# Sparse attention's first query units in float32, its modulation row formed in the feed-forward stages, the residual update in the head loop, and new planner costs

## The chip, the cores and the metric

The kernel runs on one core of one Trainium2 chip, as one launch. The metric is the device time of that launch in microseconds (us), lower is better. One core has a matrix engine (PE; its weight loads are listed as PEld), a vector engine (DVE), a scalar engine (ACT), a general engine (POOL), and a sync engine (SP) whose queue starts the transfers (DMA) from main memory (HBM). PE reads its operands from the on-chip buffer SBUF and adds into the accumulator PSUM.

## The reference, cut to what matters

Two networks in a row on 256 tokens of width 1024. The first has two layers with modulation and post-norm; the second has four layers with pre-norm (two of them forgetting attention, "fox", one gated linear attention, "gla", one gated delta net, "gdn").

```python
def first_block(x, c, ada_w, ada_b, ...):
    cond = silu(c)
    for i in range(2):
        mod = cond @ ada_w[i] + ada_b[i]                 # 6 rows of 1024
        sh1, sc1, gt1, sh2, sc2, gt2 = split(mod, 6)
        hin = x * (1 + sc1) + sh1
        y = rwkv7_time_mix(hin, ...) if i == 0 else dsa_attention(hin, ...)
        x = layernorm(ALPHA * x + (1 + gt1) * y, ln_g[i, 0], ln_b[i, 0])
        hin = x * (1 + sc2) + sh2
        x = layernorm(ALPHA * x + (1 + gt2) * swiglu(hin, ...), ln_g[i, 1], ln_b[i, 1])

def dsa_attention(h, ...):                               # sparse attention
    q, ckv, q_idx, k_idx, w_idx = split(h @ w_in)
    score = einsum(w_idx, relu(q_idx . k_idx)), causal
    idx = top_k(score, 64)                               # of 256 keys
    p = softmax((q w_uk) . ckv[idx] / 8 + rel_bias)      # 16 heads
    return ((p ckv[idx]) w_uv) @ w_out

def gdn_mixer(x, ...):                                   # 4 query/key, 8 value heads, chunks of 64
    q, k, v, z, b, a = split(x @ w_in)                   # q, k, v through a causal convolution and silu
    # decayed delta rule by chunks: the inverse of a triangular matrix of k k^T, then q k^T with the state
    return (rms_norm(o) * silu(z)) @ w_out
```

## The kernel before

**A planner inside the program.** The functions below don't issue instructions: each adds an operation to `Prog` (L346), with its possible engines and a cost in ns for each (L538 for ACT, L565 for two-input operations, L671 for copies). `schedule()` then plays all engines forward by these costs, gives every operation an engine and a buffer, and the instructions are emitted on each engine in the planned order. What order and engine an operation gets is thus decided by costs, priorities (`prog.pri`: a higher number goes later) and free buffers. Most large tiles, among them the raw weights `raw`, the split weights `whl`, the float32 inputs `xraw` and the rows `lrgb`, share one pool of 18 slots of 8 KB per partition.

**Weight units.** The token side is held transposed (features on partitions, 256 tokens in the free dimension). `ws` (L730s) makes 256 output features from a unit of 1 MB of weights: one DMA `raw`, two casts to the fp32r type (`whl<-raw`, L667 on ACT or L671 on POOL), two subtractions on DVE that give the low parts (`whl<-raw,whl`, L677), then 48 matmuls of 128x256 in three passes (high x high, high x low, low x high). `ws_full` does the same unit in plain float32: 16 matmuls straight from `raw` and the float32 input `xraw`, with no cast and no subtraction (the trace lists each float32 matmul as two). `as_proj` is the other form (512 output columns at a time) used for the projections at the end of a stage; with `turn` the two halves of the columns are computed one after the other.

**Stages**, in program order, with their place in the trace: rwkv to 262 us; its projection and layernorm to 284; feed-forward 0 to 476 (`ffi0` to 368, `ffo0` behind it); sparse attention (`dsa`) 476 to 600; layernorm 600 to 634; feed-forward 1 634 to 800; fox 835 to 931; gla 954 to 1049; gdn 1049 to 1207; fox 1226 to 1321; the last projection to 1366.

**Modulation.** `ada(l, g)` (L878) forms two rows of 1024 of `mod`, half by half: per half 8 DMAs of 512 KB (`adaraw`) and 8 DVE operations of 128x1024 (`adaacc`), then a sum over partitions on PE (`adaps`) and one small DVE operation (`adab`). `ada(1, 2)` gives `sc2` and `gt2` of layer 1, with priority 500, and is called just ahead of `dsa`.

**Sparse attention.** A projection gives scores' inputs; eight pairs of small matmuls `ix`, ACT's relu `rl` and DVE's weighted sum `dw` give the score; eight rounds of MAX8 and MATCH_REPLACE8 on DVE, for two blocks of tokens, rank it and leave the mask `selm`. Beside this, PE makes the first two query units (`d_q`), the values `vev` and the keys `kal`. The head loop (k = 0 to 7, two heads each) then adds the mask to the logits (`lgt<-selm,identb`), forms softmax on DVE, ACT and POOL (`hw`), transposes (`pT`) and multiplies (`op`); at k = 4 the query units 2 and 3 are put in, and PE goes on to the projection `do` where the heads leave room. `flush` (before the first `d_q` unit) runs the residual update of the layernorm before: four DVE operations of 128x1024 (`xr<-...,lrgb`).

**gdn.** `n_q` has eight units (0, 1 queries; 2, 3 keys; 4 to 7 values); each goes through a convolution on DVE and ACT (`cu`, `nqk` or `nvf`) and silu. `qk_unit(0)` makes the keys' matrix; `tri_inv` inverts it by a chain of about 60 small DVE operations (`tbtm`, `adtt`) and then matmuls (`iP`, `iT`, `iN`); `as_full` (`asf`) is a gate's half in float32; `qk_unit(1)` makes the query matrix (units 0 and 1 are float32 already); `solve` (`sol`) needs the inverse and the transposed values (`nvt`).

## Time and profile before

| | before |
|---|---|
| runs, us | 1363.64, 1368.45, 1355.5 (median 1363.64) |
| profiled execution, us | 1367.71 |
| its span in the trace, us | 1365.7 (2.0 less: start and end outside the span) |
| PE busy | 1283.6 us, 94% of the span |
| DVE, ACT, POOL busy | 988.7, 493.3, 363.3 us |
| mean granted clock of PE | 0.972 of full speed |

The trace gives for each instruction its engine, line, tile, start and duration, and for each idle stretch what ended it. A window row gives each engine's busy time in a stretch of the span, the clock that the throttle granted to PE (1.00 is 2.4 GHz, 0.50 is 1.2 GHz) and the mean busy share of the 16 DMA engines. The chain of work follows back from the last instruction of a stretch, at each step to what released it.

### The profile page before, as it was taken

The page shows a single profiled execution, that of the slowest core. Times are in us where ns is not written, and L with a number is a line of the kernel's source. Part 1 is how long each engine was busy: PE and PEld are TensorE (multiplying, and loading weights), DVE is VectorE, ACT ScalarE, POOL GpSimd, SP SyncE. Part 2 cuts the span into 40 slices and gives each one's busy share as a digit, 9 for nine tenths or more (in the row PEclk, how much of TensorE's full clock was granted, in tenths as well). Part 3 has the DMA queues.
Part 4 walks back from the last instruction along what each step waited for, and adds up shares of the span by engine and source line. Part 5 has one row for each costly group of instructions (what it writes and reads, how often), then busy time and mean ns, then how long its engine had stood idle before and what let it go on. Part 6 is the DMA issues. An engine that isn't in the chain of part 4 may idle for free.

```text
span 1365.7 us, 21660 instructions
## 1 busy us (share of the span) xinstructions
PE 1283.6 (94%) x8691; PEld 1087.2 (80%) x8691; DVE 988.7 (72%) x1510; ACT 493.3 (36%) x914; POOL 363.3 (27%) x355
## 2 busy tenths in 40 slices
PE   5998999998999998989999979999999996889998
PEld 2774788778998776768999859997887975768997
DVE  8699767779989688667755396467587769876563
ACT  2552212232322234543223133453243646523442
POOL 1131001311223322542421033334232311333331
PEclk9898799999999998999999999999999998999999
DMA  9565622587988563355545455424345231345510
GB/s 389 202 225 205 234 76 88 176 297 291 358 355 317 150 259 124 111 179 216 221 164 208 154 185 195 148 78 158 125 162 187 102 117 64 139 159 191 174 64 31
DMA packets 47204, 248.46 MB, mean 182 GB/s; under 512 B 5488, under 2 KB 10992, under 8 KB 23936
## 3 DMA queue, kind: packets, MB, share of 16 engines
q1 hardware_dynamic: 47104, 247.08, 50.0%
q8 instruction: 68, 1.11, 0.3%
q14 instruction: 32, 0.26, 0.1%
HBM read 240.77 MB, written 1.05 MB: 177 GB/s over the span
## 4 chain that ended last, share of the span: by engine, by line
PE 65%; DVE 18%; DMA 7%; issue 5%; POOL 3%; ACT 2%; SPq 0%; POOLq 0%; DVEq 0%; ACTq 0%
PE ws L531 28%; PE fo L531 11%; DVE whl L677 4%; PE fv L531 3%; PE lo L531 2%; DVE adaacc L580 2%; DVE tbtm L571 2%; DMA adaraw<-in_ada_w 2%; DVE adtt L571 2%; PE do L531 2%; PE flg L531 1%; DVE z L580 1%; PE asf L531 1%; PE lv L531 1%; PE Y L531 1%
## 5 line engine op out<-in xcount | busy, mean ns | idle before, releaser
L677 DVE TENSOR_TENSOR whl<-raw,whl 128x1024 fp32r<-128x1024 f32 x302 | 389.0, 1307 | 84.4 <-ACT whl L667 58.2
L531 PE MATMUL ws<-xhi,whl 128*128 128x256 f32 x2368 | 431.4, 283 | 6.3 <-DVE whl L677 4.0
L671 POOL TENSOR_SCALAR whl<-raw 128x1024 fp32r<-128x1024 f32 (+1 forms) x191 | 244.1, 1283 | 627.2 <-PE ws L531 103.5
L531 PEld LDWEIGHTS ws<-xhi,whl 128*128 128x128 f32 x2368 | 369.5, 190 | 11.3 <-DVE whl L677 4.4
L531 PE MATMUL ws<-xlo,whl 128*128 128x256 f32 x1184 | 336.0, 284 | 0.0
L531 PEld LDWEIGHTS ws<-xlo,whl 128*128 128x128 f32 x1184 | 225.0, 190 | 1.1 <-issue 1.0
L667 ACT CAST whl<-raw 128x1024 fp32r<-128x1024 f32 x111 | 114.8, 1040 | 138.0 <-DMA raw<-in_ffi 33.8
L580 DVE SCALAR_TENSOR_TENSOR adaacc<-adaraw,cond,adaacc 128x1024 f32<-128x1024 f32 x70 | 93.3, 1333 | 7.7 <-DMA adaraw<-in_ada_w 7.3
L531 PE MATMUL fo<-whl,hid 128*128 128x512 f32 x336 | 78.9, 395 | 0.4 <-DVE whl L677 0.4
L531 PEld LDWEIGHTS fo<-whl,hid 128*128 128x128 f32 x336 | 62.9, 188 | 15.3 <-DVE whl L677 0.9
L531 PE MATMUL ws<-z,raw 128*128 128x256 f32 x256 | 58.9, 383 | 0.0
L531 PEld LDWEIGHTS ws<-z,raw 128*128 128x128 f32 x256 | 47.6, 190 | 9.9 <-issue 3.5
L576 POOL TENSOR_SCALAR hw<-hw 128x128 f32<-128x128 f32 x64 | 32.0, 513 | 70.1 <-DVE hw L599 68.5
L531 PE MATMUL fv<-whl,xhi 128*128 128x512 f32 x128 | 43.1, 414 | 6.1 <-DVE whl L677 6.1
L552 ACT ACTIVATE sg<-ws 128x256 f32<-128x256 f32 x36 | 13.8, 384 | 96.1 <-PE ws L531 96.1
L531 PE MATMUL fo<-whl,hidh 128*128 128x512 f32 x192 | 44.8, 394 | 0.0
L531 PE MATMUL fa<-whl,xhi 128*128 128x512 f32 x128 | 41.7, 400 | 2.3 <-DVE whl L677 2.2
L531 PEld LDWEIGHTS fo<-whl,hidh 128*128 128x128 f32 x192 | 35.9, 188 | 8.2
L531 PE MATMUL fo<-whl,xhi 128*128 128x512 f32 x128 | 41.3, 404 | 0.0
L531 PEld LDWEIGHTS fv<-whl,xhi 128*128 128x128 f32 x128 | 25.4, 199 | 13.3 <-DVE whl L677 7.4
L531 PE MATMUL asf<-raw,z 128*128 128x512 f32 x64 | 33.2, 674 | 0.0
L571 DVE TENSOR_TENSOR hf<-sg,ws 128x256 f32<-128x256 f32 x36 | 14.9, 415 | 24.3 <-ACT sg L552 24.1
(519 smaller groups left out, 2280.0 us busy)
## 6 DMA issues: line engine op xcount, KB each, us to landing
adaraw<-in_ada_w SPq DMA_DIRECT2D x80, 512.0 KB, 6.5
raw<-in_ffi SPq DMA_DIRECT2D x36, 1024.0 KB, 6.7
raw<-in_f_q SPq DMA_DIRECT2D x24, 1024.0 KB, 5.1
raw<-in_ffo SPq DMA_DIRECT2D x20, 1024.0 KB, 6.9
adaraw<-in_ada SPq DMA_DIRECT2D x8, 1024.0 KB, 15.2
raw<-in_ffa SPq DMA_DIRECT2D x8, 1024.0 KB, 5.1
raw<-in_f_v SPq DMA_DIRECT2D x8, 1024.0 KB, 5.6
raw<-in_f_o SPq DMA_DIRECT2D x8, 1024.0 KB, 4.9
```

Source lines behind the costliest of these rows:

```text
L531: self.p.add({"PE": (c / 2.4 * share, lambda e: e.matmul(_r(o), _r(lhsT), _r(rhs), start=start, stop=stop))}, [lhsT, rhs, after] + ([] if ...
L552: lambda e: e.activation(_r(o), _r(i), f, **{k: _r(v) for k, v in kw.items()}))},
L571: self._add(c, lambda e: e.tensor_tensor(_r(o), _r(a), _r(b), op), [a, b], [o])
L576: self._add(70 + k * o.size + 60 * _ptrs(s1, s2), lambda e: e.tensor_scalar(_r(o), _r(i), _r(s1), _r(s2), **kw), [i, s1, s2], [o])
L580: self._add(70 + 1.04 * o.size + 60 * _ptrs(s), lambda e: e.scalar_tensor_tensor(_r(o), _r(a), _r(s), _r(b), op0, op1, **{k: _r(v) for k, ...
L667: alts["ACT"] = (act_cost(o, i), lambda g: g.copy(_r(o), _r(i)))
L671: alts["POOL"] = (80 + 1.0 * o.size, lambda g: g.tensor_scalar(_r(o), _r(i), 1.0, 1.0, ALU.mult, ALU.mult))
L677: alts["DVE"] = (70 + 1.04 * o.size, lambda g: g.tensor_tensor(_r(o), _r(a), _r(b), ALU.subtract))
```

## The change

Seven edits:
1. Planner costs: an ACT operation with an accumulated sum 97 ns dearer, POOL's power function dearer, POOL's copies 1.7 instead of 1.0 ns per element.
2. `as_proj` with `turn` and no `cut`: all weights of the first half of the columns are loaded ahead of those of the second.
3. `ada` can be called for one half; its bias tile is 256 wide. The `sc2` half of `ada(1, 2)` is called ahead of feed-forward 0, the `gt2` half inside feed-forward 1; nothing of it is left ahead of `dsa`.
4. Feed-forward 0's layernorm also writes its output in float32 (`xraw`, four ACT copies of 128x512); the first two `d_q` units are `ws_full`.
5. The residual update reads `lrgb` from a second load of 1 MB; `flush` in `dsa` moves from ahead of the first `d_q` unit to k = 4 of the head loop, where it is bound to the head loop's first output `Y[0][:, 0]` (its load, too).
6. gdn: units 2, 3, decays, `qk_unit(0)`, units 4, 5, `tri_inv`, then units 0, 1, 6, 7 all in float32 ahead of `qk_unit(1)`; before, units 6 and 7 were three-pass and came behind it.
7. `rmsnorm`'s first block uses the tile of the operation before it where one is handed on.

```diff
 def act_cost(o, i, ptr=0, acc=False):
-    return 95.0 + 0.833 * o.size + 93.0 * ptr + (93.0 if acc else 0.0)
+    return 95.0 + 0.833 * o.size + 93.0 * ptr + (190.0 if acc else 0.0)
...
-            c = 300 + 164.0 * o.size if op == ALU.pow else 80 + 2.25 * o.size
+            c = 1150 + 115.0 * o.size if op == ALU.pow else 80 + 2.25 * o.size
...
-            alts["POOL"] = (80 + 1.0 * o.size, lambda g: g.tensor_scalar(...))
+            alts["POOL"] = (80 + 1.7 * o.size, lambda g: g.tensor_scalar(...))
...
         both = list(enumerate(halves))
+        if turn and not cut:
+            for h in halves:
+                for k in range(0, nk, 4):
+                    load(k, (h,))
...
-    def ada(l, g, after=None, low=0):
+    def ada(l, g, after=None, low=0, parts=(0, 1)):
...
-        for h in range(2):
+        for h in parts:
+            m = cp_.tile([128, 256], F32, name="adab", ...)
+            SP.dma_start(m, d["ada_b"][l, g, :, 256 * h:256 * h + 256])
+            mods[l, names[h]] = m
...
     def layernorm(l, s, fold):
...
             x = new_x()
+            if s and not l:
+                x += (v3(big("xraw"), 8, 256),)
...
-                to_feat(b, n, x[0], x[1])
+                to_feat(b, n, x[0], x[1], raw=x[2] if len(x) > 2 else None)

                 def residual():
-                    V.scalar_tensor_tensor(xbox[0][:, b], t, mean, rgb[:, 0], ALU.add, ALU.mult)
-                    V.scalar_tensor_tensor(xbox[0][:, b], xbox[0][:, b], rstd, rgb[:, 1], ALU.mult, ALU.add)
+                    if not again:
+                        again.append(v3(big("lrgb"), 2, 1024))
+                        rows_of(d["lnrow"][2 * l + s], 2, again[0])
+                    V.scalar_tensor_tensor(xbox[0][:, b], t, mean, again[0][:, 0], ALU.add, ALU.mult)
+                    V.scalar_tensor_tensor(xbox[0][:, b], xbox[0][:, b], rstd, again[0][:, 1], ALU.mult, ALU.add)
...
         flush(hid[1][:, 2])
+        if l:
+            ada(1, 2, hid[1][:, 2], 150, (1,))
         ws(d[f"ffi{l}"], range(4, NH - 4), x, use)
...
-        flush(dl[:, 1])
-        ws(d["d_q"], range(2), x, use)
+        ws_full(d["d_q"], range(2), x[2], use)
...
             if k == 4:
                 ws(d["d_q"], range(2, 4), x, use)
+                flush(Y[0][:, 0])
...
         def qk_unit(z):
-            if z:
-                ws_full(d["n_q"], range(u0, u0 + 2), x[2], use)
-            else:
-                ws(d["n_q"], range(u0, u0 + 2), x, use)
-            if not z:
-                decays()
...
+        ws(d["n_q"], range(2, 4), x, use)
+        decays()
         qk_unit(0)
         ws(d["n_q"], range(4, 6), x, use)
         tri_inv(M01, 16, -1)
         tok_keep(as_full(d["n_z"], 8, x[2], 1), "nz", t=zt, halves=(1,))
+        ws_full(d["n_q"], range(2), x[2], use)
+        ws_full(d["n_q"], range(6, 8), x[2], use)
         qk_unit(1)
-        ws(d["n_q"], range(6, 8), x, use)
...
+    ada(1, 2, None, 300, (0,))
     out_ = ffn(0, x)
     x = lnorm(0, 1, out_, (1, 1))
-    ada(1, 2, None, 500)
     out_ = dsa(x)
```

Since the planner writes the order, the rows that it gives for each engine tell more than the diff. DVE's order at the end of the ranking in sparse attention, first the kernel before (`m` is the eight largest, `dw` the score):

```order
L580 SCALAR_TENSOR_TENSOR adaacc<-adaraw,cond,adaacc 128x1024
L596 MATCH_REPLACE dw<-m_4423,dw 128x128
L593 MAX m_4435<-dw 128x8
L576 TENSOR_SCALAR selm<-dw 128x128
L596 MATCH_REPLACE dw<-m_4435,dw 128x256
L571 TENSOR_TENSOR selm<-selm,cmaskb 128x128
L593 MAX m_4446<-dw 128x8
L677 TENSOR_TENSOR whl<-raw,whl 128x1024
L596 MATCH_REPLACE dw<-m_4446,dw 128x256
L677 TENSOR_TENSOR whl<-raw,whl 128x1024
L593 MAX m_4480<-dw 128x8
L580 SCALAR_TENSOR_TENSOR adab<-adaps,adab 128x256
```

and of the change:

```order
L596 MATCH_REPLACE dw<-m_4301,dw 128x128
L596 MATCH_REPLACE dw<-m_4303,dw 128x256
L593 MAX m_4309<-dw 128x8
L593 MAX m_4312<-dw 128x8
L596 MATCH_REPLACE dw<-m_4309,dw 128x128
L596 MATCH_REPLACE dw<-m_4312,dw 128x256
L576 TENSOR_SCALAR selm<-dw 128x128
L576 TENSOR_SCALAR selm<-dw 128x256
L571 TENSOR_TENSOR selm<-selm,cmaskb 128x128 x2
L677 TENSOR_TENSOR whl<-raw,whl 128x1024 x3
```

Between the first score operation and the last `selm`, five `adaacc`, four `whl` (two of them behind the rows shown) and the `adab` no longer stand there; in all eight rounds of the change there are only rows of the ranking. The same engine in the head loop of the change:

```order
L677 TENSOR_TENSOR xlo<-op,xhi 128x256
L580 SCALAR_TENSOR_TENSOR xr<-lnt,lns,lrgb 128x1024 x2
L677 TENSOR_TENSOR xlo<-op,xhi 128x256
L580 SCALAR_TENSOR_TENSOR xr<-xr,lns,lrgb 128x1024 x2
L571 TENSOR_TENSOR hw<-lgt,rb_4145 128x128
L571 TENSOR_TENSOR hw<-lgt,rb_4145 128x256
```

The four residual operations now stand ahead of the softmax rows (`hw`) of head 8; before, they stood ahead of the first score row. On SP's queue the `lrgb` load stands ahead of the first two weight loads of the projection `do` in the change; before, the four `d_o` loads stood in front of any `lrgb`:

```order
L618 DMA raw<-in_d_q 128x2048 x2
L618 DMA lrgb<-in_lnrow 128x2048
L618 DMA raw<-in_d_o 128x2048 x2
L618 DMA lrgb<-in_lnrow 128x2048
L618 DMA gtr<-adab 128x1x256 x4
L618 DMA raw<-in_d_o 128x2048 x2
```

PE's order in gdn, around the first matmuls that wait for DVE's inversion chain (`iP<-tbtm`), in the kernel before:

```order
L531 MATMUL nz_9681<-whl,xlo 128x512
L535 MATMUL nvt<-cst,nvf 128x128 x8
L531 MATMUL ws<-xhi,whl 128x256
L531 MATMUL ws<-xlo,whl 128x256
L531 MATMUL iP<-tbtm,M_9176 32x32 x32
L531 MATMUL nss<-sqh,onesr 128x512
L531 MATMUL iT<-tbtm,adtt 32x32
L531 MATMUL ws<-xhi,whl 128x256 x2
L531 MATMUL ws<-xlo,whl 128x256
```

and of the change:

```order
L531 MATMUL asf_9658<-raw,xraw 128x512
L531 MATMUL ws<-xraw,raw 128x256 x56
L531 MATMUL iP<-tbtm,M_9118 32x32 x32
L531 MATMUL ws<-xraw,raw 128x256 x3
L531 MATMUL iT<-tbtm,adtt 32x32 x32
L531 MATMUL iN<-adtt,tbtm 32x32 x3
L531 MATMUL ws<-xraw,raw 128x256 x4
L531 MATMUL iN<-adtt,tbtm 32x32 x13
L531 MATMUL ws<-xraw,raw 128x256
L531 MATMUL nss<-sqh,onesr 128x512
```

Before, 32 float32 matmuls (units 0 and 1) stand some rows ahead of this piece and the three-pass matmuls of units 6 and 7 behind `iP`; in the change all 64 float32 matmuls (units 0, 1, 6, 7) stand around it, 56 of them in front. Over the whole program the change has 192 three-pass matmuls fewer and 64 float32 ones more, 8 DVE subtractions of weights fewer, 28 casts of weights moved from POOL to ACT (ACT 110 to 138; POOL 188 to 152, with the 8 that fall away), and four ACT copies and three DMAs of 1 MB (`lrgb`) more.

## Rows read from the trace of the kernel before

**Rows 1.** The page: busy time and share of an engine; the chain that ended last.

```profile
PE 1283.6 (94%) x8691; PEld 1087.2 (80%) x8691; DVE 988.7 (72%) x1510; ACT 493.3 (36%) x914; POOL 363.3 (27%) x355
PE 65%; DVE 18%; DMA 7%; issue 5%; POOL 3%; ACT 2%; SPq 0%; POOLq 0%; DVEq 0%; ACTq 0%
```

**Rows 2.** Windows: from:to length, busy of PE PEld DVE ACT POOL, clock, DMA share, GB/s.

```profile
284.00:368.00 84.00, 79.18 (x594) 73.99 (x592) 76.65 (x81) 23.54 (x37) 15.06 (x12) 0.98 0.88 331
526.00:531.20 5.20, 1.31 (x17) 0.69 (x16) 5.08 (x10) 0.79 (x1) 0.00 (x0) 0.96 0.01 2
530.00:541.00 11.00, 9.86 (x39) 5.22 (x39) 7.79 (x29) 3.06 (x12) 1.65 (x4) 0.54 0.00 1
634.00:734.00 100.00, 100.00 (x850) 100.00 (x849) 69.56 (x80) 26.98 (x48) 32.58 (x25) 1.00 0.52 186
1112.00:1143.30 31.30, 21.82 (x97) 17.23 (x95) 29.14 (x66) 8.95 (x14) 5.20 (x7) 0.92 0.28 102
1143.30:1152.00 8.70, 5.97 (x80) 5.13 (x81) 8.70 (x17) 7.24 (x14) 0.24 (x1) 0.50 0.01 2
1152.00:1180.20 28.20, 23.85 (x296) 22.01 (x294) 24.58 (x41) 18.83 (x39) 8.86 (x7) 1.00 0.48 169
```

**Rows 3.** Chain of waits through sparse attention: start us, us, engine, tile and line.

```profile
499.35 2.39 DVE xr L580 x2
501.74 0.20 DVE dw L564
...
511.19 1.18 DVE adaacc L580
...
521.58 1.61 DVE adaacc L580
...
530.87 0.23 DVE selm L571
531.10 0.04 issue
531.14 7.88 PE lgt L531 x30
...
552.45 3.08 POOL whl L671 x3
```

**Rows 4.** Groups of instructions, 476 to 531: shapes, count | busy us, mean ns | idle.

```profile
L531 PE MATMUL ix<-dw,qi 64*128 64x128 f32 (+1 forms) x32 | 5.1, 486 | 1.2 <-DVE dw L564 1.2
...
L531 PE MATMUL kal<-dw,uk 128*128 128x256 f32 x16 | 3.6, 379 | 0.0
L531 PE MATMUL vev<-uv,dw 128*128 128x512 f32 x8 | 3.6, 592 | 0.0
...
L547 ACT CAST xhi<-trn 128x512 fp32r<-128x512 f32 x2 | 1.1, 582 | 0.0
```

**Rows 5.** PE in order of time, end of the ranking, then gdn: start, us, [idle before].

```profile
531.14 0.58 PE L531 MATMUL lgt<-selm,identb 128*128 128x256 bf16 x2 [3.89 <-DVE selm L571]
...
1115.45 13.98 PE L531 MATMUL ws<-xraw,raw 128*128 128x256 f32 x64
...
1143.40 1.92 PE L531 MATMUL iP<-tbtm,M 32*32 32x32 f32 x64 [7.36 <-DVE tbtm L590]
```

**Rows 6.** Chain of waits through gdn: start us, us, engine, tile and line.

```profile
1079.55 8.24 PE ws L531 x70
...
1147.86 1.13 DVE whl L677
...
1166.68 3.49 DVE whl L677 x3
...
1180.22 0.49 PE sol L531 x2
```

**Rows 7.** The page's costliest groups: count | busy us, mean ns | idle, releaser.

```profile
L671 POOL TENSOR_SCALAR whl<-raw 128x1024 fp32r<-128x1024 f32 (+1 forms) x191 | 244.1, 1283 | 627.2 <-PE ws L531 103.5
...
L667 ACT CAST whl<-raw 128x1024 fp32r<-128x1024 f32 x111 | 114.8, 1040 | 138.0 <-DMA raw<-in_ffi 33.8
```

23 lines of the change are left out of this document (10 added, 13 removed).

## The prediction

> **What bounds the kernel now.** Read the page first. PE is busy 94% of the span and carries 65% of the chain that ended last, DVE 18% [rows 1]. An average over stages doesn't say what an edit is worth, so the windows come next. In a stage like 634 to 734 PE is busy 100.00 of 100.00 us with DVE at 69.56 [rows 2]: there nothing gains unless PE gets less to do, and extra DVE work is free as long as it fits. In 284 to 368 PE, DVE (76.65 of 84) and the transfers (0.88 of the DMA engines) are all near full [rows 2]. The hollows are elsewhere, and two of them are where this change works.
>
> The first is the end of the ranking in sparse attention. In the chain of waits DVE runs from the residual update (499.35) through score and ranking to the mask `selm` at 530.87, and PE's `lgt` starts only then [rows 3]. Inside this run stand operations that have nothing to do with the ranking: five `adaacc` (the first 1.18 us, the last 1.61 [rows 3]) and four `whl`. PE idles 3.89 us for `selm` [rows 5]. What follows costs as much again: in 530 to 541 PE is busy 9.86 of 11 us at a granted clock of 0.54, that is nearly all of it at the lower level, 1.2 GHz [rows 2], and the 7.88 us of `lgt` [rows 3] lie in it. Before it, in 526 to 531.2, PE was busy 1.31 of 5.20 us [rows 2].
>
> The second is gdn. While DVE runs its inversion chain (1112 to 1143.3, busy 29.14 of 31.3) PE is busy 21.82 us [rows 2]; 7.36 us of the idle time is one wait, for the chain's end [rows 5]. Then PE runs 8.7 us at 0.50, and to 1180.2 it is busy 23.85 of 28.2 [rows 2]. The first pair of the second solve stands at 1180.22 [rows 6]. PE's idle time in 1112 to 1180.2 is 9.48 + 2.73 + 4.35 = 16.6 us.
>
> **The price of a float32 unit.** Sixty-four records of float32 matmuls, two units, take 13.98 us [rows 5]: 7.0 us a unit. Three-pass matmuls come at 8.24 / 70 = 0.118 us each [rows 6], so a unit of 48 costs 5.65 us. Float32 costs PE 1.35 us more per unit, and saves two DVE subtractions of about 1.13 [rows 6] and two casts. The Trainium skill ("FP8 and Floating Point Precision", TensorE Precision Notes) speaks against float32 on a PE-bound kernel: it says that true float32 takes four passes through the array. Four passes for three would be an estimated 7.5 us a unit; the trace's 7.0 is a little kinder, and by the page the sum below would come out some 2 us worse.
>
> **Sparse attention.** (1) `selm` no longer waits for five `adaacc` (6.4 us), four `whl` (4.5, at the 1.13 of the row in gdn [rows 6]) and one small `adab`: DVE would have it about 11 us earlier, near 520 [rows 3]. (2) PE then is late next. From the copy at 501.74 [rows 3] it owes 5.1 for the score matmuls `ix`, 14.0 for the two float32 units (2.7 more than before), and 3.6 each for `vev` and `kal` [rows 4]: 26.3 us, to about 528, well behind 520, so that `lgt` follows without a gap. So of the 11 us on DVE, PE takes 3.89 (the gap), less 2.7 of float32, and the low clock behind the gap: 11 x (1 - 0.54) = 5.1 us, which I take as gone because the clock fell behind a stretch in which PE was nearly idle, and that stretch goes. With 0.6 for the `adaps` matmuls that leave PE: -3.9 - 5.1 + 2.7 - 0.6 = -6.9. (3) The copy `dw` on which the score matmuls wait stood behind an `xr` pair until 501.74 [rows 3]; without it, -1 (bounds 0 and -2.4, the pair). (4) The four `xraw` copies are 0.58 each, by the row of the same shape [rows 4]; one of them on the path of the layernorm ahead: +0.6 (bounds 0 and 2.3). (5) In the head loop four `xr`, 2.39 a pair [rows 3], stand ahead of head 8's softmax, 4.8 us of DVE. PE has `do` and `d_q` matmuls to lay beside it, and before it idled there itself for casts on POOL (3.08 us at 552.45 [rows 3]), which is likely to shrink with fewer POOL casts. I take +1 (bounds -3 and +5). Sum: -6.3.
>
> **gdn.** PE gets 28 us of float32 matmuls that need neither cast nor DVE, and 56 of the 64 stand ahead of `iP`. Two of these units were there before; the other two fill the 9.5 us of gaps and keep PE at work up to the chain's end, so the lower clock in 1143.3 to 1152 should go (5.97 busy at half clock, 3 us). Two bounds. By PE: all idle time gone (16.6), 3.0 of clock gained, 2.7 paid for float32, about -17. By DVE: behind the chain it is busy 8.70 + 24.58 = 33.3 of the 36.9 us to 1180.2 [rows 2]; the four subtractions of units 6 and 7 (two of them 1.13 to 1.15 [rows 6]) leave, 28.7 stay, so -8.2 if all of it must come ahead of the second solve. Of it, 3.49 + 2.3 are weights of the projection behind (`whl` at 1166.68 and after [rows 6]), which the solve doesn't need. I take -10, nearer to DVE's bound since DVE is the fuller engine (bounds -4, where ACT or the output weights take over, and -14). Late next are ACT, 18.83 of 28.2 in the last window [rows 2], and the output weights' transfer.
>
> **The rest.** `gt2`'s eight `adaacc` (about 10 us of DVE, 4 MB) go under a PE at 100% with DVE at 70% [rows 2]: 0 (bounds 0 and +1); without that cover they would cost 10. The second `lrgb` load puts 1 MB in a stretch with the transfers at 0.88 and 331 GB/s [rows 2], 3 us of transfer: +1 (0 and +3). The other two `lrgb` loads fall in stretches with room. The 28 casts go from POOL, 1.28 us each, to ACT, 1.04 each [rows 7]; ACT gets 29 us over the whole span at 36% busy [rows 1]: 0 (-3 and +3). The order of loads in `as_proj` and the shorter `rmsnorm` tile use: 0 (-1 and +1).
>
> **Sum.** -6.3 - 10 + 1 = -15.3. The profiled execution took 1367.7, so a profiled 1352.4. It lies 4.1 above the median 1363.64 of the runs, which themselves spread over 13 us; against the median this is **1348**.
>
> **Rivals.** *Half of gdn.* The chain behind the inversion has other links: `nqk` on DVE, the square and exponent steps on ACT, the output weights. If these hold the solve, the -10 becomes -4: 1354. For it: DVE is busy all of 8.70 us right behind the chain [rows 2]. Against: four DVE operations leave exactly there. *Sparse attention gives it back in the head loop.* The second `lrgb` load waits in SP's queue for the first head's output, and two `d_o` loads stand behind it; PE's filler for the head loop is late, and with four `xr` ahead of the softmax PE idles up to 5 us and falls to the lower clock, as it did at 530 for another 5: the -6.3 becomes about +1, and the total 1355. For it: the 3.08 us of casts on the chain in that loop [rows 3] show that PE has no spare filler. Against: those weights are read only behind the `d_q` units. *The clock doesn't come back.* The lower clock follows a stretch of little PE work; if the gaps only move (PE waits for `vev`'s inputs, or for a `raw` slot), 8 us of the gain go: 1356. *The other side.* ACT works its queue in order. A cast on ACT that stands ahead of a softmax or layernorm step delays it by 1.04 us [rows 7], where on POOL it delayed nothing; with 28 of them moved the most is 29 us. Once 15 of them lie on the path, the gain is gone; at all 28 the time is 1348 + 29 = 1377. For it: PE waits for casts in many places. Against: most stages have PE at or near 100% and ACT under a third busy [rows 2].
>
> **How the numbers follow.** About what a measurement of this kernel can tell from no change is 1%, 13.6 us: faster means below 1350. The forecast (1340 to 1351) gets 0.50; gdn at -14 and a head loop at -3 together, near 1338, 0.08; half of gdn 0.15; sparse attention given back 0.10; the clock 0.08; ACT's casts or other reordering 0.09. Of the forecast's 0.50 nearly all lies below 1350. So faster 0.55, within 1% 0.36, slower 0.09. The range reaches from 1336 to 1363, which leaves out the most lucky sum and the casts.
>
> **What would show it.** Right: `selm` near 520 and `lgt` behind `kal` without a gap; clock 1.00 in the head loop's first 10 us; PE over 95% busy in the inversion chain; the second solve 10 us after where it would be less. Wrong: `lgt` still waiting for `selm`; a new gap of PE ahead of head 8's softmax; `iP` or `nG` waiting for DVE with PE empty; ACT's `whl` as releaser of PE's idle time where POOL's stood before. Most likely to break the forecast is gdn, where the largest term rests on what is late next.

## The result, and the profile after

The changed kernel takes 1346.64 us (median of four runs, 1341.88 to 1354.08) against 1364.82 for the kernel before in the same comparison: a ratio of **0.9878, 95% interval 0.9851 to 0.9905**, 16.6 us less (13 to 20). The forecast was 1348. The profiled execution took 1348.87 us, with a span of 1347.1.

On the page of the changed kernel PE's share rises from 94 to 96%, and PE's part of the chain that ended last from 65 to 77%; DVE's falls from 18 to 14% [rows 1].

```profile
PE 1291.1 (96%) x8627; PEld 1091.8 (81%) x8627; DVE 971.8 (72%) x1502; ACT 523.4 (39%) x952; POOL 336.6 (25%) x313
...
PE 77%; DVE 14%; DMA 3%; POOL 2%; issue 2%; ACT 1%; SPq 0%; DVEq 0%; POOLq 0%; ACTq 0%
```

The windows of the changed kernel that answer to [rows 2], in the same columns: the first feed-forward's units; sparse attention from its input to the last `kal`, the first logits, two stretches of the head loop; gdn's inversion chain and what follows to the first solve.

```profile
296.80:406.30 109.50, 107.28 (x901) 104.69 (x900) 97.07 (x107) 29.76 (x52) 28.58 (x17) 0.98 0.88 326
478.00:519.80 41.80, 39.07 (x198) 31.64 (x197) 24.39 (x85) 15.23 (x31) 4.55 (x5) 0.96 0.36 143
519.80:531.00 11.20, 11.20 (x91) 8.19 (x89) 8.81 (x32) 7.05 (x20) 2.46 (x6) 1.00 0.09 23
531.00:550.00 19.00, 19.00 (x147) 15.68 (x145) 6.20 (x14) 8.87 (x30) 6.87 (x12) 1.00 0.64 236
550.00:569.00 19.00, 18.05 (x76) 10.69 (x74) 18.12 (x45) 11.65 (x35) 9.00 (x12) 0.82 0.40 127
1104.90:1130.50 25.60, 24.21 (x116) 21.00 (x115) 23.68 (x59) 6.47 (x13) 1.36 (x3) 1.00 0.44 161
1130.50:1157.60 27.10, 24.24 (x296) 20.42 (x297) 21.42 (x46) 21.33 (x46) 9.12 (x5) 0.81 0.23 78
```

Two places are as the prediction said: PE is busy all of the first logits' 11.2 us at full clock, and 24.21 of 25.60 us (95%) beside the inversion chain. Two are not: 550 to 569 has a clock of 0.82, and the stretch behind the chain 0.81.

A trace is one execution. The kernel before with only gdn changed (an experiment below) gives a second one of the same sparse attention: up to gdn each of its compute engines runs the same instructions in the same order as in the kernel before. From the end of `kal` to the first `op` of the head loop it takes 15.30 us at a clock of 0.89, where the trace of the kernel before has 18.40 at 0.72. Second execution, then the kernel before:

```profile
525.50:540.80 15.30, 11.76 (x86) 7.17 (x83) 13.29 (x43) 5.99 (x18) 2.22 (x6) 0.89 0.02 3
524.90:543.30 18.40, 14.51 (x84) 8.81 (x82) 13.96 (x43) 5.94 (x18) 2.47 (x6) 0.72 0.07 18
```

So 3 us of any difference to the trace of before at this place can be the execution and not an edit.

The chain of waits through the change's sparse attention, which answers to [rows 3]: PE carries it alone from the score matmuls to 549, and then the residual update `xr` stands on it.

```profile
495.82 3.08 PE ix L531 x18
498.90 14.01 PE ws L531 x64
512.91 3.43 PE vev L531 x8
516.35 3.45 PE kal L531 x16
519.80 6.28 PE lgt L531 x48
...
551.12 2.39 DVE xr L580 x2
553.51 0.53 DVE hw L571 x2
```

**Two parts of a time.** Each run comes with its span and its mean granted clock. Runs of one kernel differ by up to 19 us, and in most kernels the larger part of that is the clock; in 53 runs of the kernel before it lies between 0.965 and 0.977. Span times (1 - clock) is what the lower level took, and span times clock is what is left; I call them *lost to the clock* and *work* below. For the kernel before work is 1321.7 us and 39.9 are lost (means of the 53). Over the runs of one kernel work scatters by 1.0 to 3.2 us (standard deviation), the span by 1.0 to 7.9; for the kernel before the two are close, 2.7 and 3.2. The table gives the standard error of each mean: for the change, of four runs only, it is 1.6 us, so a difference of 2 us in work to the change is within the noise. Nor is work quite free of the clock: within the kernels, one us more lost goes with 0.76 us more of span. For the changed kernel work is 1313.2 and 32.3 are lost: half of the gain, 8.5 us, is work, and 7.6 us are clock. Two of the six runs of the kernel with the update at k = 6 below (1351.1 and 1352.6 us, clock 0.967) count as slow and are left out of its row; with them its median is 1345.9, its work 1306.3, and 36.1 are lost.

### The profile page after: what moved, and what is told of

The parts are those of the page before. It is cut to its first block, busy times and chain, and to the rows that moved or that the text cites. A ratio compares the mean times of both kernels' runs of the same rounds, so it can differ in the third digit from the quotient of the medians.

```text
span 1347.1 us, 21507 instructions
## 1 busy us (share of the span) xinstructions
PE 1291.1 (96%) x8627; PEld 1091.8 (81%) x8627; DVE 971.8 (72%) x1502; ACT 523.4 (39%) x952; POOL 336.6 (25%) x313
## 3 DMA queue, kind: packets, MB, share of 16 engines
HBM read 243.92 MB, written 1.05 MB: 182 GB/s over the span
## 4 chain that ended last, share of the span: by engine, by line
PE 77%; DVE 14%; DMA 3%; POOL 2%; issue 2%; ACT 1%; SPq 0%; DVEq 0%; POOLq 0%; ACTq 0%
PE ws L531 33%; PE fo L531 12%; PE fa L531 3%; PE fv L531 2%; PE lo L531 2%; DVE whl L677 2%; PE ro L531 2%; PE lv L531 2%; DVE adtt L571 2%; DVE tbtm L571 2%; PE flg L531 1%; DVE z L580 1%; PE no L531 1%; PE lz L531 1%; PE Y L531 1%
## 5 line engine op out<-in xcount | busy, mean ns | idle before, releaser
L677 DVE TENSOR_TENSOR whl<-raw,whl 128x1024 fp32r<-128x1024 f32 (+2 forms) x294 | 377.6, 1304 | 71.8 <-ACT whl L667 49.9
L531 PE MATMUL ws<-xhi,whl 128*128 128x256 f32 x2240 | 406.6, 282 | 2.2 <-ACT whl L667 1.5
L671 POOL TENSOR_SCALAR whl<-raw 128x1024 fp32r<-128x1024 f32 (+2 forms) x154 | 211.2, 1375 | 609.8 <-DMA raw<-in_ffi 90.5
L531 PEld LDWEIGHTS ws<-xhi,whl 128*128 128x128 f32 x2240 | 347.7, 189 | 7.0 <-issue 2.8
L531 PE MATMUL ws<-xlo,whl 128*128 128x256 f32 x1120 | 317.0, 283 | 0.0
L531 PEld LDWEIGHTS ws<-xlo,whl 128*128 128x128 f32 x1120 | 211.7, 189 | 0.8 <-issue 0.6
L667 ACT CAST whl<-raw 128x1024 fp32r<-128x1024 f32 x140 | 142.9, 1035 | 115.3 <-DMA raw<-in_ffo 30.6
L552 ACT ACTIVATE sg<-ws 128x256 f32<-128x256 f32 x36 | 13.9, 385 | 118.4 <-PE ws L531 118.4
L531 PE MATMUL ws<-z,raw 128*128 128x256 f32 x256 | 58.9, 383 | 0.0
L531 PEld LDWEIGHTS ws<-z,raw 128*128 128x128 f32 x256 | 47.6, 190 | 9.9 <-issue 3.5
L576 POOL TENSOR_SCALAR hw<-hw 128x128 f32<-128x128 f32 (+1 forms) x64 | 35.2, 564 | 77.4 <-DVE hw L599 52.5
L531 PE MATMUL fo<-whl,hidh 128*128 128x512 f32 x192 | 44.8, 394 | 0.0
L531 PE MATMUL ws<-xraw,raw 128*128 128x256 f32 x192 | 42.7, 381 | 0.0
L531 PEld LDWEIGHTS fo<-whl,hidh 128*128 128x128 f32 x192 | 35.9, 188 | 8.3
L531 PEld LDWEIGHTS ws<-xraw,raw 128*128 128x128 f32 x192 | 36.1, 190 | 5.6 <-issue 0.5
```

What stands on the lines that cost most here:

```text
L531: self.p.add({"PE": (c / 2.4 * share, lambda e: e.matmul(_r(o), _r(lhsT), _r(rhs), start=start, stop=stop))}, [lhsT, rhs, after] + ([] if ...
L552: lambda e: e.activation(_r(o), _r(i), f, **{k: _r(v) for k, v in kw.items()}))},
L576: self._add(70 + k * o.size + 60 * _ptrs(s1, s2), lambda e: e.tensor_scalar(_r(o), _r(i), _r(s1), _r(s2), **kw), [i, s1, s2], [o])
L667: alts["ACT"] = (act_cost(o, i), lambda g: g.copy(_r(o), _r(i)))
L671: alts["POOL"] = (80 + 1.7 * o.size, lambda g: g.tensor_scalar(_r(o), _r(i), 1.0, 1.0, ALU.mult, ALU.mult))
L677: alts["DVE"] = (70 + 1.04 * o.size, lambda g: g.tensor_tensor(_r(o), _r(a), _r(b), ALU.subtract))
```

## The experiments

All runs in one table; ratios are to the kernel before on the same chip, and work and lost are means over a kernel's runs. A number behind ± is a standard error, here and below.

| kernel | median us | ratio, 95% interval | work | lost to the clock |
|---|---|---|---|---|
| before | 1363.3 to 1365.0 | 1 | 1321.7 ± 0.4 | 39.9 |
| the change | 1346.6 | 0.9878 (0.9851 to 0.9905) | 1313.2 ± 1.6 | 32.3 |
| before + planner costs | 1364.5 | 0.9994 (0.9967 to 1.0021) | 1318.9 ± 0.7 | 42.8 |
| before + modulation | 1361.0 | 0.9982 (0.9958 to 1.0006) | 1320.0 ± 0.6 | 39.0 |
| before + whole sparse-attention part | 1356.6 | 0.9942 (0.9922 to 0.9963) | 1318.7 ± 0.4 | 35.9 |
| before + gdn | 1358.3 | 0.9953 (0.9930 to 0.9975) | 1319.2 ± 0.6 | 37.5 |
| change, costs of before | 1350.7 | 0.9908 (0.9879 to 0.9938) | 1315.9 ± 1.1 | 34.1 |
| change, gdn of before | 1357.2 | 0.9950 (0.9923 to 0.9977) | 1315.3 ± 0.7 | 40.3 |
| change, first query units in three passes | 1338.6 | 0.9829 (0.9794 to 0.9863) | 1310.9 ± 0.8 | 27.5 |
| change, update ahead of the ranking | 1353.8 | 0.9913 (0.9881 to 0.9944) | 1312.3 ± 0.5 | 36.6 |
| change, update behind the head loop | 1353.9 | 0.9911 (0.9871 to 0.9950) | 1313.1 ± 1.2 | 36.3 |
| change, update at k = 6, bound to the mask | 1340.7 | 0.9830 (0.9784 to 0.9877) | 1306.7 ± 0.9 | 31.8 |
| both corrections | 1336.0 | 0.9782 (0.9753 to 0.9811) | 1306.2 ± 1.0 | 26.4 |
| both, one gdn unit held back | 1343.9 | 0.9850 (0.9823 to 0.9877) | 1305.1 ± 0.5 | 36.9 |

### One part at a time

The planner's costs alone:

```diff
-    return 95.0 + 0.833 * o.size + 93.0 * ptr + (93.0 if acc else 0.0)
+    return 95.0 + 0.833 * o.size + 93.0 * ptr + (190.0 if acc else 0.0)
...
-            c = 300 + 164.0 * o.size if op == ALU.pow else 80 + 2.25 * o.size
+            c = 1150 + 115.0 * o.size if op == ALU.pow else 80 + 2.25 * o.size
...
-            alts["POOL"] = (80 + 1.0 * o.size, ...)
+            alts["POOL"] = (80 + 1.7 * o.size, ...)
```

> The kernel before with the three planner costs of the change alone. Prediction's theory (the gain sits in sparse attention and gdn; the costs are worth 0, bounds -3 and +3): 1361 to 1368, ratio 0.998 to 1.002. Rival, from the change's trace, where the stages up to the end of the first feed-forward already end 7 us earlier and the layernorms and first projections behind them some more: the costs alone give 5 to 10 us, ratio 0.993 to 0.996, and the gain shows in the stretches up to 480 us and in the layernorm stages, not in sparse attention or gdn.

Measured 0.9994. In time the prediction's 0 holds, and the rival's 5 to 10 us fall. In work the costs are worth 2.8 us (1321.7 to 1318.9, ± 0.8), given back to the clock in these runs (42.8 lost).

The reverse, the change with the costs of before:

```diff
-    return 95.0 + 0.833 * o.size + 93.0 * ptr + (190.0 if acc else 0.0)
+    return 95.0 + 0.833 * o.size + 93.0 * ptr + (93.0 if acc else 0.0)
...
-            c = 1150 + 115.0 * o.size if op == ALU.pow else 80 + 2.25 * o.size
+            c = 300 + 164.0 * o.size if op == ALU.pow else 80 + 2.25 * o.size
...
-            alts["POOL"] = (80 + 1.7 * o.size, ...)
+            alts["POOL"] = (80 + 1.0 * o.size, ...)
```

> The changed kernel with the planner's costs of before. Prediction's theory (the costs are worth 0): same as the change, 1345 to 1349. Rival (alone they took 2.8 us off the span times clock while losing as much to the clock): span times clock 1315 to 1317, time 1348 to 1352.

Work 1315.9, 2.7 (± 2.0) more than the change, inside the rival's 1315 to 1317: by itself not clear of the noise, but the same size from the other side. So the costs do carry something in work, at the edge of the prediction's bound of -3, and not the "0" that it took.

The sparse-attention part alone (modulation by halves, float32 input and units, second `lrgb` load, update at k = 4):

```diff
+    ada(1, 2, None, 300, (0,))
     out_ = ffn(0, x)
     x = lnorm(0, 1, out_, (1, 1))
-    ada(1, 2, None, 500)
...
-        flush(dl[:, 1])
-        ws(d["d_q"], range(2), x, use)
+        ws_full(d["d_q"], range(2), x[2], use)
...
             if k == 4:
                 ws(d["d_q"], range(2, 4), x, use)
+                flush(Y[0][:, 0])
```

> The kernel before with the sparse-attention part alone: modulation by halves, float32 input and first two query units, residual update in the head loop. Prediction's theory: -6.3 there and +1 for the second load, about 1359, ratio 0.996; the chain from the start of the score to the first op of the head loop about 10 us shorter and the head loop no longer than before. Rival (the head loop gives it back): ratio 0.999 to 1.002; the first logits 10 us earlier, but the end of do at most 2 us earlier, with the four xr on the chain of waits ahead of head 8's softmax.

Measured 1356.6, ratio 0.9942: by the time the prediction is right. By the place it isn't. The first logits do start early, but the head loop's last `op` and the end of `do` stand no nearer to the start of the stage than before (118.1 us from the last transpose of the layernorm ahead to the last `do`, against 118.4; 116.0 in the second execution of the same instructions as before). Place and path are the rival's, then, and the time is not. In this execution time was gained ahead of the stage: the stretch from the last `Y` of the first stage to the last `fa` is 49.0 us instead of 52.8, and the first feed-forward's units take 104.9 instead of 111.6, of which 4.0 come back until that last transpose (75.0 instead of 71.0).

The modulation alone:

```diff
-    def ada(l, g, after=None, low=0):
+    def ada(l, g, after=None, low=0, parts=(0, 1)):
...
         flush(hid[1][:, 2])
+        if l:
+            ada(1, 2, hid[1][:, 2], 150, (1,))
...
+    ada(1, 2, None, 300, (0,))
     out_ = ffn(0, x)
...
-    ada(1, 2, None, 500)
```

> The kernel before with the modulation edit alone (formed by halves, gt2's half inside feed-forward 1). Prediction's theory: its 11 us of DVE operations leave the ranking, PE's gap there shrinks by 3.9 and the lower clock behind it goes: -4 to -8, ratio 0.994 to 0.997, and nothing changes in the first feed-forward. Rival (from the traces of the change and of the sparse-attention part alone, whose first feed-forward units are 2 to 7 us shorter than in the kernels without it): a like gain, but from 300 to 410 us, where fewer adaacc stand between the weight subtractions on DVE, and at most 2 us up to the end of do.

The ratio, 0.9982, leaves 0 to 6 us. The trace shows the mechanism as predicted, and free of the other edits; the rival's place, the first feed-forward, gains nothing (112.4 us for its units in this trace, 111.6 in that of before). Windows of this kernel: the score and the ranking, the first logits, the head loop.

```profile
482.40:524.80 42.40, 36.70 (x225) 30.13 (x225) 33.66 (x93) 16.15 (x32) 9.98 (x7) 0.96 0.46 174
524.80:536.70 11.90, 11.90 (x96) 8.79 (x94) 7.55 (x31) 6.55 (x19) 2.48 (x6) 1.00 0.14 36
536.70:581.50 44.80, 44.44 (x291) 32.90 (x290) 24.66 (x65) 24.40 (x76) 25.20 (x34) 1.00 0.47 147
```

From the end of `kal` to the first `op` are 11.9 us at full clock; in the trace of before it was 18.40 us at 0.72, in the second execution 15.30 at 0.89 (rows in the section on the result). The head loop behind it was:

```profile
543.30:590.60 47.30, 46.75 (x310) 35.02 (x309) 23.90 (x64) 23.35 (x75) 27.11 (x36) 1.00 0.43 139
```

That is 6.5 us at this place, or 3.4 against the second execution, and the head loop is no longer (44.8 against 47.3). So the modulation alone brings in its place most of what the prediction gave to the whole part. The median shows some 2.5 us of it, and the interval reaches to 6.

gdn alone:

```diff
-            if z:
-                ws_full(d["n_q"], range(u0, u0 + 2), x[2], use)
-            else:
-                ws(d["n_q"], range(u0, u0 + 2), x, use)
-            if not z:
-                decays()
...
+        ws(d["n_q"], range(2, 4), x, use)
+        decays()
         qk_unit(0)
         ws(d["n_q"], range(4, 6), x, use)
         tri_inv(M01, 16, -1)
         tok_keep(as_full(d["n_z"], 8, x[2], 1), "nz", t=zt, halves=(1,))
+        ws_full(d["n_q"], range(2), x[2], use)
+        ws_full(d["n_q"], range(6, 8), x[2], use)
         qk_unit(1)
-        ws(d["n_q"], range(6, 8), x, use)
```

> The kernel before with the reordered gdn alone (query units first float32, units 6 and 7 float32, before the second matrix). Prediction's theory: -10, about 1354, ratio 0.993. Rival (half of gdn, another link holds the solve): -4 to -6, ratio 0.996 to 0.997, with the second solve 4 to 6 us nearer to the start of the stage.

Measured 0.9953, 6.4 us (3.4 to 9.5): just above the rival's 4 to 6, and the interval leaves the 10 out. And the change without it:

```diff
         def qk_unit(z):
             u0 = 0 if z else 2
+            if z:
+                ws_full(d["n_q"], range(u0, u0 + 2), x[2], use)
+            else:
+                ws(d["n_q"], range(u0, u0 + 2), x, use)
+            if not z:
+                decays()
...
-        ws(d["n_q"], range(2, 4), x, use)
-        decays()
         qk_unit(0)
...
-        ws_full(d["n_q"], range(2), x[2], use)
-        ws_full(d["n_q"], range(6, 8), x[2], use)
         qk_unit(1)
+        ws(d["n_q"], range(6, 8), x, use)
```

> The changed kernel with gdn as before (units 6 and 7 in three passes behind the query matrix). Prediction's theory: gdn is worth 10, so about 1356, ratio 0.994 to 0.996. From the run of gdn alone (ratio 0.9953, -6.4): about 1352 to 1353, ratio 0.991 to 0.993.

Measured 1357.2: in the change gdn is worth 10.6 us of the median, or 5 to 15 by the two ratios, as the prediction had it. Its work is 2.5 us (± 0.7) alone and 2.1 (± 1.7) in the change; the rest in the change is clock (40.3 lost instead of 32.3). The traces say what the reorder does each time. In the five kernels with the old order (before, costs, modulation, sparse attention, and this one) PE is busy 15.8 to 16.1 us of the last 25.5 of the inversion chain, at a clock of 0.86 to 0.90; in the eight with the new order (without the last one below, which holds a unit back) 24.0 to 24.4 us, at 1.00 each time. From the last transpose ahead of gdn to the end of its output projection the five take 156.9 to 161.8 us, the eight 143.6 to 155.9.

### Where the head loop gave it back

In the change the stretch from the first `op` to the last is 51.7 us (531.5 to 583.1), against 47.3 before. PE in order of time there, changed kernel:

```profile
548.75 0.49 PE L531 MATMUL lgt<-kal,qve 64*128 64x128 f32 x4
...
551.19 0.48 PE L531 MATMUL lgt<-kal,qve 64*128 64x128 f32 x2
...
551.82 0.70 PE L531 MATMUL lgt<-kal,qve 64*128 64x256 f32 x2
...
559.86 2.82 PE L531 MATMUL op<-hw,qve 128*64 128x128 f32 x12
```

Up to 549 four `lgt<-kal` records (two heads, 64 rows each, side by side in the array) take 0.49 us; from 551 two records take 0.48: four heads go one by one, and each pair costs twice. I read it so, from the order and not from a run of its own: the softmax's first addition `hw`, which frees a logits buffer in PSUM, stands behind the four `xr` on DVE, so the planner has buffers for one head at a time. That `xr` causes it is not shown, since the kernel with the planner's costs alone has four such heads too, with no `xr` in its head loop. Then the clock falls: the twelve `op` at 559.86 take 2.82 us, where six take 0.80 at full clock elsewhere in the loop. PE was busy all of 554 to 560 while the clock went from 1.00 to 0.50.

DVE starts the second pair of `xr` at 551.12 and the softmax of head 8 at 553.51 (chain above). It had been busy only 6.20 of the 19 us before (531 to 550). The `lrgb` load is not what holds the pairs: it is issued at 529.13, before the first `op` (531.5), and has landed at 533.6.

```profile
529.13 0.33 SPq L618 DMA_DIRECT2D lrgb<-in_lnrow  x1
...
544.47 0.43 DVE L677 TENSOR_TENSOR xlo<-op,xhi 128x256 fp32r<-128x256 f32 x1 [0.83 <-ACT xhi L547]
544.81 3.03 DVE L580 SCALAR_TENSOR_TENSOR xr<-lnt,lns,lrgb 128x1024 f32<-128x1024 f32 x2
550.69 0.42 DVE L677 TENSOR_TENSOR xlo<-op,xhi 128x256 fp32r<-128x256 f32 x1 [2.85 <-ACT xhi L547]
```

It is DVE's planned order. The binding of `flush` to the first output holds in the plan alone, which puts the first pair behind three `xlo` and the second behind a fourth. The `xlo` wait for the heads' `op` on PE, and the softmax of head 8 stands behind them all. All five traces with the update at k = 4 show the loss: from the first `op` to the last `do` they take 64.1 to 69.8 us, at a clock of 0.90 to 0.93 in the head loop; the nine others take 56.4 to 60.0, at 0.97 to 1.00.

Three other places for the update tell what a place costs. Behind the head loop:

```diff
-                flush(Y[0][:, 0])
...
+        flush(Y[0][:, 6])
         return as_proj(d["d_o"], xl(Y), 8, "do", 8 - TAIL, turn=True)
```

> The changed kernel with the residual update of sparse attention bound to the seventh output of the head loop instead of standing at k = 4, so that its four operations fall under the last matmuls of the projection. Prediction's theory (the update in the head loop costs about 1): same as the change, 1345 to 1348, ratio to before 0.987 to 0.988. Rival (the four xr ahead of head 8's softmax hold the head loop, PE's logits matmuls are then issued one head at a time and the clock falls): 5 to 7 us better than the change, 1340, ratio 0.983 to 0.985, no stretch of clock 0.50 in the head loop.

Measured 0.9911, 1353.9: not better. The last `do` is 109.2 us behind the layernorm ahead of the stage instead of 116.9, as the rival has it, but the layernorm behind takes 17.9 instead of 9.0. Its chain of waits shows why:

```profile
587.39 4.47 DVE xr L580 x4
...
598.38 5.78 issue
...
604.19 1.47 POOL lns L571
```

The four `xr` now stand between the steps of the next layernorm, which is as much on the path as the softmax. They are 4.5 of the 8.9 us; the 5.78 us ahead of POOL's `lns` stay without a cause in the trace.

Ahead of the ranking, where it was before the change (with the second load):

```diff
+        flush(dl[:, 1])
         ws_full(d["d_q"], range(2), x[2], use)
...
-                flush(Y[0][:, 0])
```

> The changed kernel with the residual update back ahead of the first query unit (second load kept), so that its four operations lie inside the ranking. DVE has selm at 513.8 in the change and PE asks for it at 519.6, so 4.8 us more of DVE fit. Theory that the update in the head loop costs about 1 (prediction): within 2 us of the change, ratio 0.986 to 0.990. Rival (in the head loop it unpairs PE's logits matmuls and lets the clock fall): 4 to 6 us better than the change, ratio 0.982 to 0.985, head loop (first op to last) near 47 us instead of 51.7.

Measured 0.9913, work 1312.3: no better than the change either. The head loop does get its time back (57.2 us from the first `op` to the last `do`, at full clock), as the rival has it. But 4.5 us are lost again from the last `do` to the last `fa` behind (31.4 instead of 26.9, at a clock of 0.89), and 0.5 ahead of the head loop. Its chain of waits, with the first and the last of four `xr` and the last of two `whl`:

```profile
505.61 1.60 DVE xr L580
...
513.84 1.19 DVE xr L580
...
520.65 1.13 DVE whl L677
...
523.28 5.80 PE lgt L531 x42
```

The ranking leads again: the logits wait for it until 523.28, 2.8 us behind the last `kal` at 520.5. The slack of 5.8 us (513.8 to 519.6 in the change) was eaten by `xr` and `whl` together.

Bound to the mask and called at k = 6:

```diff
-                flush(Y[0][:, 0])
+            if k == 6:
+                flush(selm[:, 128:384])
```

> The changed kernel with the residual update bound to the mask instead of the head loop's first output and called at k = 6: the planner spreads the four operations singly over DVE's free time in the first half of the head loop, and the logits matmuls are planned in pairs for all but one head. Theory that the update in the head loop costs about 1: within 2 us of the change. Rival: 4 to 7 us better than the change, ratio 0.981 to 0.985, without the 17.9 us layernorm of the kernel with the latest update.

Measured 0.9830 (0.9784 to 0.9877), work 1306.7: 6.5 us (± 1.8) less work than the change. The planner spreads the four operations singly over 527 to 537, where DVE has waits anyway. The head loop and the projection behind it, then the same of the change:

```profile
527.00:573.30 46.30, 46.09 (x296) 34.12 (x296) 30.64 (x69) 25.67 (x77) 30.61 (x33) 1.00 0.56 190
573.30:583.90 10.60, 10.59 (x45) 8.27 (x45) 8.96 (x15) 5.50 (x7) 3.36 (x3) 1.00 0.29 99
```
```profile
531.50:583.10 51.60, 50.59 (x292) 36.17 (x291) 31.38 (x68) 25.02 (x75) 27.67 (x33) 0.93 0.51 167
583.10:595.60 12.50, 12.46 (x58) 9.92 (x58) 10.30 (x18) 6.04 (x9) 4.65 (x4) 1.00 0.50 168
```

56.9 us instead of 64.1, with the clock at 1.00 instead of 0.93. So the update in the head loop, as the change has it, costs about 7 us in its place: 3.4 of them are the lower clock, 0.8 idle time of PE, and the rest, 3, is what is left for the unpaired logits. In this execution 3.8 us come back in the layernorm and projection behind (30.7 instead of 26.9), where the clock is 0.79 for 16 us; over the runs the work stands for a gain of 6.5.

### The price of float32

The first two query units back in three passes (`xraw` still written):

```diff
-        ws_full(d["d_q"], range(2), x[2], use)
+        ws(d["d_q"], range(2), x, use)
```

> The changed kernel with the first two query units back in three passes (xraw still written). Prediction's theory: PE saves 2.7 us, DVE gets four subtractions (4.5 us) and casts back; with the modulation out of the way DVE is at 513.8 + 4.5, still ahead of PE: 0 to -2 against the change, ratio 0.986 to 0.989. Rival (float32 is what keeps PE fed at the start of the ranking, where the three-pass units wait for casts): PE idles and the clock falls near 500, +3 to +6, ratio 0.990 to 0.993.

Measured 1338.6, 8 us better than the change, which neither side expected; the intervals of the two ratios (0.9794 to 0.9863 and 0.9851 to 0.9905) overlap by a little. Work falls by 2.3 us (± 1.8), near the 2.7 that the prediction worked out as float32's price (2 x 1.35) and not clear of the noise. The other 5 are clock: 27.5 us lost instead of 32.3. The stage itself is no shorter in this trace (127.2 us from the last `fo` of the feed-forward to the last `do`, 126.6 in the change), and 7.7 of the 11.9 us between the two traces lie in gdn, where PE's order came out another. The two units do get cheaper, 12.44 us instead of 14.01, but the projection ahead of them ends 1.4 us later behind the last `fo`, and `ix` runs in part at the lower clock. The kernel of both corrections, which also leaves out the copies `xraw`, shows the price without that. Three passes, then both corrections:

```profile
492.25 4.21 PE ix L531 x20
496.46 12.44 PE ws L531 x96
```
```profile
491.73 2.22 PE ix L531 x20
493.95 11.37 PE ws L531 x96
```

There the first `op` stands 56.5 us behind the last `fo`, and 62.5 in the change and in the kernel with the update at k = 6: 6 us for units and copies together, some of it clock (1.00 instead of 0.96 up to the last `kal`). `selm` is ready 3.7 us ahead of the last `kal`, so DVE had room for the four subtractions, and here float32 only costs.

### Both corrections, and a look at gdn's clock

```diff
-        ws_full(d["d_q"], range(2), x[2], use)
+        ws(d["d_q"], range(2), x, use)
...
-                flush(Y[0][:, 0])
+            if k == 6:
+                flush(selm[:, 128:384])
...
-            if s and not l:
-                x += (v3(big("xraw"), 8, 256),)
```

> The changed kernel with both corrections: sparse attention's first query units in three passes (no xraw written), and the residual update bound to the mask and called at k = 6. Taken as span times mean granted clock, the change stands at 1313, the two corrections alone at 1311 and 1306. If they add: 1304, and with the 27 to 36 us that the lower clock takes in these kernels a time of 1331 to 1342, ratio 0.975 to 0.983. If they overlap (three passes put whl subtractions back into DVE's free time, which the residual update needs): 1308 to 1311, no better than either alone, ratio 0.983 to 0.986.

Measured 1336.0, ratio **0.9782 (0.9753 to 0.9811)**: the best of all, 10 us under the change and inside the 1331 to 1342 for corrections that add. In work they don't (1306.2, as with the update alone, where 1304 was expected), although the trace has sparse attention 6 us shorter than with the update alone; the rest is clock (26.4 lost). Why work doesn't show these 6 stays open.

What the clock does in gdn is seen in four kernels in which the compute engines' instructions between the chain's end and the first solve stand in the same order. Update at k = 6; update behind the head loop; three passes; both:

```profile
1120.20:1147.50 27.30, 27.26 (x280) 22.61 (x281) 18.04 (x35) 16.22 (x31) 7.31 (x4) 0.62 0.18 55
```
```profile
1139.60:1159.40 19.80, 19.78 (x281) 16.71 (x282) 16.89 (x35) 16.26 (x31) 7.31 (x4) 0.91 0.24 80
```
```profile
1126.40:1145.10 18.70, 18.27 (x281) 15.64 (x282) 16.39 (x35) 16.21 (x31) 7.80 (x4) 1.00 0.26 83
```
```profile
1121.20:1139.90 18.70, 18.26 (x280) 15.62 (x281) 16.35 (x35) 16.21 (x31) 7.78 (x4) 1.00 0.26 86
```

The same work takes 27.3 us at 0.62, 19.8 at 0.91 and 18.7 at 1.00. In the first PE is busy for 27.26 of 27.30 us, and in the 25.5 us ahead of it for 24.2, as in the others. Its clock falls at 1122.0, 1.8 us into the stretch, when PE had run the first 32x32 matmuls of the inverse behind an idle 1.34 us:

```profile
1120.20:1122.00 1.80, 1.76 (x67) 1.69 (x68) 1.80 (x6) 1.75 (x4) 0.00 (x0) 0.99 0.05 14
1122.00:1142.40 20.40, 20.40 (x181) 16.36 (x180) 11.46 (x23) 11.73 (x23) 3.33 (x3) 0.50 0.15 53
```

The two kernels at 1.00 have the same gap (1.36 and 1.40 us) and the same matmuls behind it. Whether the clock falls on these small matmuls was the next question: unit 1's float32 matmuls are held until the chain ends, so that they lie among them (edit to the kernel of both corrections).

```diff
-    def ws_full(src, units, x, use):
+    def ws_full(src, units, x, use, after=None):
...
-        tri_inv(M01, 16, -1)
+        tn = tri_inv(M01, 16, -1)
...
-        ws_full(d["n_q"], range(2), x[2], use)
-        ws_full(d["n_q"], range(6, 8), x[2], use)
+        ws_full(d["n_q"], range(6, 8), x[2], use)
+        ws_full(d["n_q"], range(1), x[2], use)
+        ws_full(d["n_q"], range(1, 2), x[2], use, tn[0:32, 0])
```

> The kernel of both corrections, and in gdn the float32 matmuls of query unit 1 held back until the inversion chain on DVE has ended, so that 16 of them lie among the 32x32 and 64x64 matmuls behind it; the query matrix then comes behind the solve. Theory that the low clock there follows from PE waiting (prediction): holding work back opens a wait of up to 7 us inside the chain, the clock falls there, +3 to +8 against the kernel of both corrections. Rival (PE is busy all through that stretch in the change and the clock falls all the same, so it is the small matmuls that it falls on): the granted clock between the end of the chain and the solve rises from 0.62 to 0.91 (mean of the kernels so far near 0.8) to over 0.9 and the time lost to the lower clock falls by 4 to 8 us; span 0 to -6.

```profile
1101.00:1126.70 25.70, 24.40 (x117) 21.14 (x116) 23.78 (x59) 6.45 (x13) 1.13 (x2) 1.00 0.41 150
1126.70:1146.30 19.60, 18.62 (x267) 15.90 (x268) 15.53 (x27) 13.35 (x24) 5.29 (x5) 0.91 0.20 70
...
1153.50:1200.20 46.70, 37.87 (x194) 31.64 (x194) 36.17 (x59) 20.24 (x41) 10.90 (x10) 0.89 0.32 113
```

Neither side gets its way. The stretch ahead of the chain's end has no new wait (24.40 of 25.70 us busy) and a clock of 1.00 (other matmuls filled it), so the first theory's wait of 7 us doesn't come; behind it the clock is 0.91, inside the spread of the kernels without the hold (0.62 to 1.00), and it falls again behind the solve (0.89). The time is 8 us worse, which is the first theory's number without its mechanism. The work is the same within the noise (1305.1 and 1306.2), so the difference is clock (36.9 lost), and not all of it in gdn. What makes the clock fall on a busy PE in one execution and not in another stays open.

## Why the prediction was right, and where it wasn't

The time, 1346.6, is within 1.4 us of the 1348 forecast, and the ratio is faster by 1.2%. So close a hit is in part luck: the sum hides terms that were off in both directions. Between the trace of before and that of the change sparse attention, counted from the last `fo` to the last `do`, gains nothing (126.6 us in both) where -6.3 was summed; gdn gains 6.1 where -10 was; and 5.3 come ahead of the feed-forward, where nothing was expected.

**Sparse attention, steps 1 and 2: the path right, the clock term too large.** `selm` is ready at 513.8, 35.1 us behind the last transpose of the layernorm ahead; before, it was 46.7 (531.1 - 484.4): 11.6 us, where about 11 were worked out. PE is late next, as said: the chain has float32 units, `vev`, `kal` and `lgt` without a gap, and the first logits' stretch is at full clock. The first `op` comes 6.1 us earlier in the stage (52.8 instead of 58.9 us), against -6.9 and -1. But the 5.1 us of lower clock were read from one execution: the second one of the same instructions has 56.5 us, so that the gain is 3.7 against it. Step 4, the copies `xraw`, was taken as +0.6: the last transpose stands 9.7 us behind the last `fo` instead of 8.2.

**Step 5, the update in the head loop: mis-sized, and the step that failed.** It was taken as +1 with bounds of -3 and +5. From the first `op` to the last `do` the change takes 64.1 us where 59.5 were before: +4.6, at the upper bound, so that the stage from its transposes on gains 1.5 us (116.9 against 118.4). With the update elsewhere in DVE's free time it is 56.9. The rival had the place (four `xr` ahead of the softmax, the clock falling behind them) and a part of the mechanism; but the `lrgb` load, which it had wait for the first head's output, had landed 11 us ahead of the first `xr`, and PE did not idle for the weights of `do`: its matmuls went on, unpaired for four heads, which neither had.

**The float32 price: right** (2.7 worked out; 2.6 in place, 14.01 us against 11.37 for the two units at full clock; 2.3 ± 1.8 as work). The Trainium skill ("FP8 and Floating Point Precision", TensorE Precision Notes) has four passes for true float32, which spoke against this edit. These rows agree in direction.

**gdn: the size right, the reason only in part.** -10 was taken; alone it gives 6.4, in the change 10.6. PE fills the inversion chain (24.21 of 25.60 us). But the step "the lower clock in 1143.3 to 1152 should go" failed: in the change the stretch behind the chain has 0.81. There the third rival has it, the gap only moves: the clock falls at 1140.1, inside a new wait of PE for `rsf` on DVE, the longest gap of the stretch.

```profile
1141.17 0.80 PE L531 MATMUL nss<-rsf,onesr 128*128 128x512 f32 x1 [2.86 <-DVE rsf L677]
```

In the kernel with the update at k = 6 it falls without such a wait, so a busy PE alone doesn't keep the clock up either. Work is only 2.1 to 2.5 us of the term.

**The rest, taken as +1: off by a sum of small gains.** The stretch from the last `Y` of the first stage to the last `fa` is 47.6 us instead of 52.8. Seven later traces with the change's costs and its sparse-attention edits have 47.5 to 47.8 there; the costs alone have 50.1, the sparse-attention part alone 49.0, the modulation alone 53.7 and gdn alone 51.9. So the costs and the sparse-attention part each bring some of it, and neither the modulation nor, since that part leaves it out, the order of loads is needed. The float32 copies and units are not needed either (47.5 in the kernel of both corrections), which leaves the second `lrgb` load; it was not run by itself. The units of the first feed-forward take 109.5 instead of 111.6, with 97.07 us of DVE instead of 103.23 (before: 301.9 to 413.5); the second execution of before has 114.4. The second load's transfer, the +1, shows nowhere. Edits 2 and 7 were never run by themselves.

**What it would have shown.** Of the signs that were named, `lgt` behind `kal` without a gap, the clock at the first logits and a full PE in the chain came; of those against, "a new gap of PE ahead of head 8's softmax" came in another form: PE was busy there with unpaired matmuls, so that its idle time showed nothing.

## What to carry to other kernels

Moving work off a chain is worth what the next engine leaves of it; but where the moved work goes decides as much: an operation that nothing needs soon belongs bound to the earliest thing that is ready and called late, so that a scheduler can put it into idle time, and not ahead of a step on the path. On a kernel bound by PE a swap to float32 pays only where it takes work from the engine that sets the end, and it stops paying as soon as another edit has relieved that engine. Where runs of one kernel spread by the granted clock, span times clock tells edits of 2 to 3 us apart that the time doesn't, given some ten runs a side. And a term read from one trace should be read again in another execution of the same instructions, above all where a low clock is part of it.
